# A decoder layer on one core: x fetched ahead of the modulation's weights, its transposes and the convolution's taps placed elsewhere

## The chip, the cores and the metric

The kernel runs as one program on one core of a Trainium2 chip. The measure is the device time of one execution in microseconds. Three runs of the kernel before gave 1677.51, 1674.44 and 1684.07 us, with a median of 1677.51 us. The execution that was profiled took 1679.29 us; its span, from the first to the last instruction in the trace, is 1677.5 us.

## The reference

One step of one decoder layer for 256 prompt rows and 64 sample rows (8 sequences of 8), 320 rows of 2048 numbers in all. Cut to what touches the change:

```python
ada = silu(c) @ w_ada + b_ada                 # c: 9 vectors of 2048; w_ada: 2048 x 12288
sh1, sc1, g1, sh2, sc2, g2 = split(ada, 6)
h = layer_norm(x) * (1 + sc1) + sh1           # x: 320 x 2048
proj = h @ w_in                               # w_in: 2048 x 7168
# S5 state-space branch and convolution branch (31 taps for each channel) on parts of proj,
# gates, an output product, a second norm, then a mixture of 32 experts, and a last norm
x = layer_norm(ALPHA * x + g1 * mix, ln1_g, ln1_b)
```

The modulation vectors `sc1` and `sh1` need 4096 of the 12288 columns of `w_ada` before `h` can be made; `layer_norm(x)` needs all of x.

## The kernel before, in words

Everything here is about the first 180 us. Work is written down as a program in Python; a scheduler then fixes the order of each engine's instructions from that order, from priorities and from its own estimate of times. On the chip each engine runs its list in that order and waits where an operand is not there.

**The four sets.** `ada_set` makes 512 columns of `sc1` and 512 of `sh1`. It reads 16 blocks of `w_ada`, 128 rows by 1024 columns, 0.524 MB each, issued on SP's queue as two DMAs of 256 KB (L279). Four matmuls at half width multiply a pair of blocks (helper line L188, tile `adp`), so a set is eight groups of two blocks; they are called group 1 to group 8 here, and the blocks of all sets are counted from 0, so that group 1 of the second set takes blocks 16 and 17. There are seven buffers for the blocks: four that rotate, named `raw`, two inside `rawu`, and `rawc`. The four `raw` buffers also hold the first slices of `w_in` (L601). A block is fetched when its buffer is free, and SP issues in the written order. At a set's end ScalarE copies `adp` out (`ae`, L304), four small products with `pair` fold it (tile `tpp`), and VectorE adds the bias into `ada` (L312).

**x.** `x_load` (L238 to L243) fetches x in three DMAs: two of 1.05 MB and one of 0.52 MB. They stand behind the first four blocks of `w_ada`. `ln0` first takes the statistics (L335) and normalises x in place (L338), then transposes it in 16 chunks of 128 columns (L346): three transposes on TensorE into a PSUM tile `s5p`, of which there are two, and one copy by ScalarE (L347) into `xnT`. The tiles of x lie in the same memory as the three big tables of the S5 setup, so that the first table (L418) waits for the last transposes.

**Beside them.** `s5_setup` makes the tables and small matrices of the S5 branch, mostly on VectorE. `taps` (L613 to L620) lays out the convolution's taps by 128 tiny matmuls from `cwn` into one `tpp` tile. `bias_rows` transposes the bias. `k_outer(k)` makes `h` of chunk k (L360 to L363, its high part on ScalarE at L368), fetches 768 columns of `w_in`, splits them in a high part (ScalarE, L542) and a low part (VectorE, L543), and multiplies them in 18 matmuls into six PSUM tiles (`acc`, `s5p`). It runs for chunks 4(q-1) to 4(q-1)+3 inside set q, and for 12 to 15 behind the last set. After that the products with `w_in` go on in blocks of 256 columns.

Of the kernel before, what the change touches and what calls it, by code (L numbers as in the profile page):

```python
# [24 lines left out]
T = SEQ + NB * TS  # L25
# [16 lines left out]
TOK = ((0, 128), (128, 128), (256, 64))  # L42
# [106 lines left out]
def bc(ap, shape):  # L149
    return ap.to_broadcast(shape)  # L150


def build(tc, A, O):
    nc = tc.nc
    V, S, GP, PE, SY = nc.vector, nc.scalar, nc.gpsimd, nc.tensor, nc.sync
# [19 lines left out]
    def acc():  # L175
        return pp.tile([128, 512], F32, name="acc", tag="acc", bufs=4)

    def s5p(name="s5p"):
        return pp.tile([128, 512], F32, name=name, tag="s5p", bufs=2)

    def tpp(name="tpp"):
        return pp.tile([128, 512], F32, name=name, tag="tpp", bufs=1)

    def stg(name="stg", shape=(128, T), dt=F32):
        return pa.tile(list(shape), dt, name=name, tag="stg", bufs=7)

    def mm(out, l, r, a, b, skip=True):
        return PE.matmul(out, lhsT=l, rhs=r, start=a, stop=b, skip_group_check=skip)  # L188
# [7 lines left out]
    ident = kc[:, C_ID:C_ID + 128]  # L196
# [41 lines left out]
    def x_load():  # L238
        for i, (t0, n) in enumerate(TOK):
            if i < 2:  # L240
                SY.dma_start(out=xt[i], in_=A["x_prompt"][0, t0:t0 + n])
            else:
                SY.dma_start(out=xt[i][:n], in_=A["x_sample"].rearrange("b s d -> (b s) d"))  # L243
# [4 lines left out]
    ps = tpp()  # L248
# [5 lines left out]
    def bias_rows():  # L254
        bn = stg("bn")
        S.dma_start(out=bn[:96, :128], in_=A["b_ada"][0].rearrange("(k p) -> k p", p=128))
        ps = tpp()
        PE.transpose(ps[:, :96], bn[:96, :128], ident[:96, :96])
        V.tensor_copy(bT, ps[:, :96])
        for part in (1, 4):  # L260
            V.tensor_scalar(bT[:, 16 * part:16 * part + 16], bT[:, 16 * part:16 * part + 16], 1.0, None, op0=OP.add)
# [30 lines left out]
    def ada_set(cols):  # L292


        ps = pp.tile([128, 512], F32, name="adp", tag="adp", bufs=1)
        for k in range(0, KT, 2):
            raws = [ada_load(cols, k + h) for h in range(2)]
            four([(ps[64 * a + 32 * h:64 * a + 32 * h + 32, :], scT[:, k + h, :], raws[h][:, 512 * a:512 * a + 512],
                   k == 0, k == KT - 2) for h, a in ((1, 1), (0, 0), (0, 1), (1, 0))])
            yield  # L300
            yield
        es = [stg("ae")[:, :256] for i in range(2)]
        for i, e in enumerate(es):
            S.copy(e, ps[:, 256 * i:256 * i + 256])  # L304
        yield
        tp = tpp()
        for i in range(4):
            mm(tp[:, 64 * i:64 * i + 64], es[i // 2][:, 128 * (i % 2):128 * (i % 2) + 128], pair, True, True)
        tv = tp[:, :256].rearrange("p (i a s) -> p a i s", i=4, a=2)
        for a, c in enumerate(cols):  # L310
            f = c // 128
            tt(ada[:, f:f + 4, :], tv[:, a, :, :NS], bc(bT[:, f:f + 4, None], [128, 4, NS]), op=OP.add)  # L312
        yield


    def rstd_(v, tmp, y):

        ts(v, v, EPS, None, op0=OP.add)
        root = S.activation(tmp, v, AF.Sqrt)
        V.reciprocal(y, tmp)  # L320
        tt(tmp, y, y, op=OP.mult)
        tt(tmp, tmp, v, op=OP.mult)
        ts(tmp, tmp, -0.5, 1.5, op0=OP.mult, op1=OP.add)
        tt(y, y, tmp, op=OP.mult)
        return root

    xnT = [pr2.tile([128, 8, T], F32, name=f"xnT{h}", tag=("Y0", "Y1")[h]) for h in range(2)]
    sdb = p0.tile([128, T], F32, name="sdb", tag="sdb")

    def ln0():  # L330
        st = stg("st")
        mv = stg("mv")
        for i, (t0, n) in enumerate(TOK):
            for c in range(4):
                V.bn_stats(st[:n, 24 * i + 6 * c:24 * i + 6 * c + 6], xt[i][:n, 512 * c:512 * c + 512])  # L335
            V.bn_aggr(mv[:n, 2 * i:2 * i + 2], st[:n, 24 * i:24 * i + 24].rearrange("p (c s) -> p c s", s=6))
            rstd_(mv[:n, 2 * i + 1:2 * i + 2], mv[:n, 16 + i:17 + i], mv[:n, 8 + i:9 + i])
            ts(xt[i][:n], xt[i][:n], mv[:n, 2 * i:2 * i + 1], mv[:n, 8 + i:9 + i], op0=OP.subtract, op1=OP.mult)  # L338

            stt(mv[:n, 24 + i:25 + i], mv[:n, 2 * i + 1:2 * i + 2], ALPHA, mv[:n, 8 + i:9 + i],  # L340
                op0=OP.mult, op1=OP.mult)
        yield
        for k in range(KT):
            ps = s5p()
            for i, (t0, n) in enumerate(TOK):
                PE.transpose(ps[:, t0:t0 + n], xt[i][:n, 128 * k:128 * k + 128], ident[:n, :n])  # L346
            S.copy(xnT[k // 8][:, k % 8, :], ps[:, :T])  # L347
            yield
        ps = tpp()
        for i, (t0, n) in enumerate(TOK):  # L350
            mm(ps[:, t0:t0 + n], bc(mv[:n, 24 + i:25 + i], [n, 128]), ident[:n, :n], True, True)
        V.tensor_copy(sdb, ps[:, :T])
        yield

    h_hi = pa.tile([128, KT, T], F32R, name="h_hi", tag="H0")
    h_lo = pa.tile([128, KT, T], F32R, name="h_lo", tag="H1")
# [241 lines left out]
    def k_outer(k):  # L598
        make_h(k)
        raw = raw_tile()  # L600
        SY.dma_start(out=raw[:, :768], in_=w_in[:, k, 0:768])  # L601
        hi, lo = split(raw[:, :768], 768)
        for m in range(6):
            mm3(first[m][:, :T], hi[:, 128 * m:128 * m + 128], lo[:, 128 * m:128 * m + 128],
                hh[0](k), hh[1](k), k == 0, k == KT - 1)
# [4 lines left out]
    def taps():  # L610
        ps = tpp()
        pick = ident[:CW, 0:32].rearrange("p (r s) -> p s r", s=4)
        for c in range(8):  # L613
            for j in range(4):
                x = 32 * c + 8 * j
                for s in range(4):
                    mm(ps[32 * s:32 * s + 32, x:x + 8], cwn[:CW, 128 * c + 32 * j:128 * c + 32 * j + 32], pick[:, s, :],
                       True, True)
        V.tensor_copy(cwS.rearrange("p c j r -> p (c j r)"), ps[:, :256])
        V.tensor_reduce(oneh, ident.rearrange("p (a c) -> p c a", a=4), axis=AX, op=OP.add)  # L620

    setup, norm = Side(s5_setup()), ln0()
    for q in range(4):
        for i, _ in enumerate(ada_set([D + 512 * q, 512 * q])):
            if q == 0:
                if i == 2:
                    x_load()
                    taps()
                if i == 3:
                    bias_rows()  # L630
                    next(norm)
                if 6 <= i < 15:
                    next(norm, None)
                    next(norm, None)
                setup.give(800)
            else:
                if i % 4 == 3 and i < 16:
                    k_outer(4 * q - 4 + i // 4)
                setup.give(1100)
# [906 lines left out]
    for c in range(4):  # L1546
        tv = [x.rearrange("p (f kk) -> p kk f", kk=4) for x in parts_of[c][:5]]
        for h in range(2):
            for kk in range(4):
                ps = acc()  # L1550
# [732 lines left out]
```

## Time and profile before

| what | value |
|---|---|
| median of three runs | 1677.51 us |
| profiled execution | 1679.29 us, span 1677.5 us |
| TensorE busy over the span | 1486.2 us, 89% |
| VectorE, ScalarE, GpSimd busy | 878.0, 550.3, 247.6 us |
| bytes over the span | 447.39 MB, mean 267 GB/s |
| mean busy share of the DMA engines, 40 to 60 us | 0.61 |
| the same, 120 to 140 us | 1.14 |

In the rows on engines the busy time of a stretch stands before the count of instructions in brackets. The DMA share is the mean over 16 engines and can pass 1 where transfers of several queues overlap. A row of a timeline gives the start, the time to the end of the last one, the engine, the line, the operation with out<-in, the number merged in the row, and in square brackets how long the engine had been idle and what ended that. TensorE records two matmuls for each 4-byte one that the program writes, so that a group of four is eight records.

### The profile page before, as it was taken

What the parts mean: (1) busy time and instruction counts of PE and PEld (TensorE: products, weight loads), DVE (VectorE), ACT (ScalarE), POOL (GpSimd) and SP (SyncE); (2) the same over time, 40 slices, a digit from 0 to 9 for tenths busy, and PEclk for the clock granted to TensorE, in tenths of its full rate; (3) what the DMA queues carried; (4) which work ended last, traced back from release to release, by engine and by line L of the source; (5) the groups of instructions that cost most, each with busy time, mean ns of one, the idle gap of its engine ahead of it and who ended that gap; (6) DMA issues with size and microseconds to landing.
All of it is one profiled execution on the core that took longest, in us unless ns stands there. A gap on an engine that the chain in (4) does not pass through costs nothing. (4 is left out here: it accounts for less than half of the span.)

```text
span 1677.5 us, 28072 instructions
## 1 busy us (share of the span) xinstructions
PE 1486.2 (89%) x10731; PEld 1039.7 (62%) x10731; DVE 878.0 (52%) x1724; ACT 550.3 (33%) x960; POOL 247.6 (15%) x419
## 2 busy tenths in 40 slices
PE   4977988998999899989799999989879997979894
PEld 1453877887777778878688988858522332323431
DVE  4564347675924853796354645463531533424365
ACT  1222433342324224523333433332231423232534
POOL 3021212134222210101100000000200000010013
PEclk9987989999999999999899999989999999989997
DMA  9799999789679976867576645555799899999992
GB/s 260 255 313 291 280 275 235 239 217 268 175 229 247 181 217 197 221 220 229 186 248 217 213 134 175 167 194 226 292 401 413 320 411 412 412 360 412 412 412 101
DMA packets 214899, 447.39 MB, mean 267 GB/s; under 512 B 23811, under 2 KB 134067, under 8 KB 206732
## 3 DMA queue, kind: packets, MB, share of 16 engines
q1 hardware_dynamic: 179572, 395.65, 67.8%
q0 software_dynamic: 29168, 43.15, 11.9%
q10 hardware_dynamic: 6016, 6.70, 1.3%
q8 instruction: 87, 1.43, 0.4%
q14 instruction: 56, 0.46, 0.1%
HBM read 425.53 MB, written 21.77 MB: 267 GB/s over the span
## 5 line engine op out<-in xcount | busy, mean ns | idle before, releaser
L543 DVE TENSOR_TENSOR wlo<-raw,whi 128x1024 fp32r<-128x1024 f32 (+1 forms) x196 | 237.6, 1213 | 304.0 <-ACT whi L542 298.8
L542 ACT CAST whi<-raw 128x1024 fp32r<-128x1024 f32 (+1 forms) x196 | 201.8, 1030 | 388.6 <-PE acc L188 231.9
L188 PE MATMUL acc<-h_hi,whi 128*128 128x320 f32 x864 | 275.9, 324 | 5.5 <-ACT whi L542 3.6
L188 PE MATMUL acc<-h_lo,whi 128*128 128x320 f32 x864 | 272.5, 318 | 0.0
L188 PE MATMUL acc<-h_hi,wlo 128*128 128x320 f32 x864 | 261.9, 322 | 5.3 <-DVE wlo L543 5.2
L188 PE MATMUL up<-ring,xg 128*32 128x512 f32 x1344 | 175.5, 610 | 11.1 <-DMA ring<-in_moe_w_gate 10.2
L188 PEld LDWEIGHTS acc<-h_hi,whi 128*128 128x128 f32 x864 | 167.3, 195 | 28.9 <-ACT whi L542 10.8
L188 PEld LDWEIGHTS acc<-h_hi,wlo 128*128 128x128 f32 x864 | 162.6, 194 | 22.1 <-DVE wlo L543 8.2
L188 PEld LDWEIGHTS acc<-h_lo,whi 128*128 128x128 f32 x864 | 167.7, 194 | 3.6 <-issue 1.4
L188 PE MATMUL adp<-raw,scT 128*32 128x512 f32 x636 | 120.7, 689 | 22.9 <-DMA raw<-in_w_ada 22.9
L188 PEld LDWEIGHTS up<-ring,xg 128*32 128x32 f32 x1344 | 42.6, 113 | 102.3 <-issue 90.3
L188 PE MATMUL pd<-ring,aT 128*32 128x512 f32 (+1 forms) x688 | 97.7, 675 | 5.9 <-DVE aT L1871 5.9
L188 PE MATMUL acc<-y_hi,whi 128*128 128x320 f32 x256 | 80.0, 315 | 6.6 <-DVE m L1010 6.6
L1927 ACT COPY z<-pd 32x512 f32<-32x512 f32 (+1 forms) x92 | 53.0, 576 | 87.3 <-PE pd L188 84.9
L1709 DVE TENSOR_TENSOR x1tok<-x1tok,acc 128x512 f32<-128x512 f32 x80 | 51.7, 683 | 56.6 <-PE acc L188 56.3
L188 PE MATMUL acc<-m_hi,whi 128*128 128x320 f32 x256 | 81.3, 319 | 0.0
L188 PE MATMUL acc<-m_lo,whi 128*128 128x320 f32 x256 | 80.2, 314 | 0.0
L188 PE MATMUL acc<-y_lo,whi 128*128 128x320 f32 x256 | 79.6, 313 | 0.0
L188 PE MATMUL acc<-m_hi,wlo 128*128 128x320 f32 x256 | 78.3, 317 | 0.0
L188 PE MATMUL acc<-y_hi,wlo 128*128 128x320 f32 x256 | 75.9, 316 | 0.0
L188 PE MATMUL acc<-vhl,whi 128*128 128x320 f32 x256 | 58.5, 324 | 2.1 <-DVE vhl L915 2.1
L1610 DVE COPY xg<-XS 128x512 f32 x34 | 14.5, 426 | 84.8 <-PE up L188 81.6
(689 smaller groups left out, 2581.2 us busy)
## 6 DMA issues: line engine op xcount, KB each, us to landing
ring<-in_moe_w_up SPq DMA_DIRECT2D x120, 512.0 KB, 11.5
ring<-in_moe_w_gate SPq DMA_DIRECT2D x120, 512.0 KB, 11.5
ring<-in_moe_w_down SPq DMA_DIRECT2D x60, 1024.0 KB, 11.6
raw<-in_w_ada SPq DMA_DIRECT2D x119, 512.0 KB, 5.3
raw<-in_w_in SPq DMA_DIRECT2D x100, 512.0 KB, 5.8
raw<-in_w_ada SPq DMA_DIRECT2D x80, 256.0 KB, 5.1
raw<-in_w_out SPq DMA_DIRECT2D x32, 512.0 KB, 4.5
rawu<-in_w_ada SPq DMA_DIRECT2D x32, 256.0 KB, 5.1
```

The lines of the kernel that those rows point to most:

```text
L188: return PE.matmul(out, lhsT=l, rhs=r, start=a, stop=b, skip_group_check=skip)
L542: S.copy(hi[:, :n], raw_ap)
L543: tt(lo[:, :n], raw_ap, hi[:, :n].bitcast(F32), op=OP.subtract)
L1610: state[g % 2] = (V.tensor_copy if g % 2 == 0 else S.copy)(xg[:, :, 32 * g:32 * g + 32], XS[:, :, bass.ds(off, 32)])
L1709: tt(x, x, o, op=OP.add)
L1927: S.copy(zs[q * ng + nb][0][s0:s0 + m_], pd[m_ * q:m_ * q + m_])
```

## The change

The call of `x_load` moves ahead of the four sets, so SP issues x before any block of `w_ada`. The order of the other DMAs on SP's queue stays. In `ln0` the three products that spread the rows' scale (`sdb`) move ahead of the transposes and lose their own step. In the first set the statistics are taken at step 2 rather than 3, one chunk is asked for at each of the steps 4 to 15 (two at each of 6 to 14 before), and the last four chunks are written in the second set's steps 0 to 4. `taps` is written behind the last group of the first set (step 16).

```diff
         yield
+        ps = tpp()
+        for i, (t0, n) in enumerate(TOK):
+            mm(ps[:, t0:t0 + n], bc(mv[:n, 24 + i:25 + i], [n, 128]), ident[:n, :n], True, True)
+        V.tensor_copy(sdb, ps[:, :T])
         for k in range(KT):
             ...
             S.copy(xnT[k // 8][:, k % 8, :], ps[:, :T])
             yield
-        ps = tpp()
-        for i, (t0, n) in enumerate(TOK):
-            mm(ps[:, t0:t0 + n], bc(mv[:n, 24 + i:25 + i], [n, 128]), ident[:n, :n], True, True)
-        V.tensor_copy(sdb, ps[:, :T])
-        yield
...
+    x_load()
     setup, norm = Side(s5_setup()), ln0()
     for q in range(4):
         for i, _ in enumerate(ada_set([D + 512 * q, 512 * q])):
             if q == 0:
                 if i == 2:
-                    x_load()
-                    taps()
+                    next(norm)
                 if i == 3:
                     bias_rows()
-                    next(norm)
-                if 6 <= i < 15:
+                if 4 <= i < 16:
                     next(norm, None)
-                    next(norm, None)
+                if i == 16:
+                    taps()
                 setup.give(800)
             else:
+                if q == 1 and i < 5:
+                    next(norm, None)
```

On VectorE all twelve statistics of x now stand ahead of the S5 setup's first operations; before, those stood ahead. The copy `sp<-tpp` of the setup, which needs a transpose that TensorE makes behind group 1, now stands between the first and the second of the three normalisations.

TensorE inside the first set, before: two transposes of a chunk, a group, and the first transposes of the chunks behind it (`xt_95` to `xt_97` are the three tiles of x).

```order
L346 MATMUL s5p<-kc,xt_96 128x128
L346 MATMUL s5p<-kc,xt_97 128x64
L188 MATMUL adp<-rawu,scT 32x512
L188 MATMUL adp<-raw,scT 32x512 x2
L188 MATMUL adp<-rawu,scT 32x512
L346 MATMUL s5p<-kc,xt_95 128x128
L346 MATMUL s5p<-kc,xt_96 128x128
L346 MATMUL s5p<-kc,xt_97 128x64
L346 MATMUL s5p<-kc,xt_95 128x128
L346 MATMUL s5p<-kc,xt_96 128x128
L346 MATMUL s5p<-kc,xt_97 128x64
```

The same place with the change:

```order
L188 MATMUL tpp<-kc,cwn 32x8 x13
L350 MATMUL s5p<-kc,xt_95 128x128
L188 MATMUL adp<-rawu,scT 32x512
L188 MATMUL adp<-raw,scT 32x512 x2
L188 MATMUL adp<-rawu,scT 32x512
L350 MATMUL s5p<-kc,xt_96 128x128
L350 MATMUL s5p<-kc,xt_97 128x64
L188 MATMUL tpp<-kc,cwn 32x8 x11
L350 MATMUL s5p<-kc,xt_95 128x128
L350 MATMUL s5p<-kc,xt_96 128x128
L350 MATMUL s5p<-kc,xt_97 128x64
L188 MATMUL tpp<-kc,cwn 32x8 x15
```

The tiny matmuls of the taps (`cwn`), which stood between groups 1, 2 and 3 before, now stand between the chunks from group 3 on, up to group 7. All sixteen chunks stand ahead of group 8 of the first set; before, fifteen did, and the last one behind it.

TensorE from the end of the first set into the second, before: the folding products with `pair`, groups 1 to 4 of the second set, then the first matmuls of chunk 0 (`h_hi,whi`).

```order
L188 MATMUL tpp<-pair,ae 128x64 x4
L188 MATMUL adp<-rawu,scT 32x512
L188 MATMUL adp<-raw,scT 32x512 x2
L188 MATMUL adp<-rawu,scT 32x512 x2
L188 MATMUL adp<-raw,scT 32x512 x2
L188 MATMUL adp<-rawu,scT 32x512
L188 MATMUL adp<-rawc,scT 32x512
L188 MATMUL adp<-raw,scT 32x512 x2
L188 MATMUL adp<-rawc,scT 32x512
L188 MATMUL adp<-raw,scT 32x512 x4
L188 MATMUL acc<-h_hi,whi 128x320 x4
L188 MATMUL s5p<-h_hi,whi 128x320 x2
```

With the change, from group 8 of the first set on:

```order
L188 MATMUL adp<-raw,scT 32x512 x4
L188 MATMUL tpp<-pair,ae 128x64 x4
L188 MATMUL adp<-rawu,scT 32x512
L188 MATMUL adp<-raw,scT 32x512 x2
L188 MATMUL adp<-rawu,scT 32x512 x2
L188 MATMUL adp<-raw,scT 32x512 x2
L188 MATMUL adp<-rawu,scT 32x512
L188 MATMUL acc<-h_hi,whi 128x320 x4
L188 MATMUL s5p<-h_hi,whi 128x320 x2
L188 MATMUL adp<-rawc,scT 32x512
L188 MATMUL adp<-raw,scT 32x512 x2
L188 MATMUL adp<-rawc,scT 32x512
```

The first six matmuls of chunk 0 now stand ahead of group 3, and twelve more of them ahead of group 4.

TensorE at the end of the fourth set, before: group 7, the folding products of the third set, group 8, and chunk 8 of `k_outer`.

```order
L188 MATMUL adp<-rawc,scT 32x512
L188 MATMUL adp<-raw,scT 32x512 x2
L188 MATMUL adp<-rawc,scT 32x512
L188 MATMUL tpp<-pair,ae 128x64 x4
L188 MATMUL adp<-raw,scT 32x512 x4
L188 MATMUL acc<-h_hi,whi 128x320 x4
L188 MATMUL s5p<-h_hi,whi 128x320 x2
L188 MATMUL tpp<-pair,ae 128x64 x4
L188 MATMUL acc<-h_lo,whi 128x320
```

With the change, from group 6 of the fourth set on:

```order
L188 MATMUL adp<-rawu,scT 32x512
L188 MATMUL adp<-raw,scT 32x512 x2
L188 MATMUL adp<-rawu,scT 32x512
L188 MATMUL tpp<-pair,ae 128x64 x4
L188 MATMUL acc<-h_hi,whi 128x320 x4
L188 MATMUL s5p<-h_hi,whi 128x320 x2
L188 MATMUL adp<-rawc,scT 32x512
L188 MATMUL adp<-raw,scT 32x512 x2
L188 MATMUL adp<-rawc,scT 32x512
L188 MATMUL acc<-h_lo,whi 128x320
L188 MATMUL acc<-h_hi,wlo 128x320
L188 MATMUL acc<-h_lo,whi 128x320
```

The folding products of the third set and the first matmuls of chunk 8 now stand ahead of group 7; group 8 stands behind all of chunks 8 and 9.

## Rows read from the trace of the kernel before

**Rows 1.** Windows of 20 us: busy (count) by engine, clock, DMA share, GB/s.

```profile
0.00:20.00 20.00, 5.96 (x86) 2.00 (x89) 4.25 (x24) 3.18 (x4) 13.49 (x23) 1.00 0.91 236
...
40.00:60.00 20.00, 20.00 (x74) 7.18 (x73) 0.75 (x2) 6.30 (x16) 0.00 (x0) 1.00 0.61 206
60.00:80.00 20.00, 16.55 (x85) 9.79 (x85) 19.96 (x28) 3.71 (x8) 0.00 (x0) 0.83 0.87 292
...
120.00:140.00 20.00, 12.72 (x75) 4.90 (x74) 3.21 (x4) 3.38 (x6) 4.05 (x7) 0.75 1.14 337
```

**Rows 2.** Waits of SP's queue, 0 to 200 us: total us, times, longest.

```profile
SPq L279 <- PE adp L188: 41.3, 21, 4.9
```

**Rows 3.** Timeline of TensorE and VectorE, 17 to 38 us, arrivals and statistics.

```profile
17.73 1.06 PE L188 MATMUL adp<-rawu,scT 128*32 128x512 f32 x1 [5.21 <-DMA rawu<-in_w_ada]
...
20.41 1.88 DVE L335 BATCH_NORM_STATS2 st<-xt 128x6 f32<-128x512 f32 x3 [5.69 <-DMA xt<-in_x_prompt]
...
25.33 0.69 DVE L335 BATCH_NORM_STATS2 st<-xt 128x6 f32<-128x512 f32 x1 [1.93 <-DMA xt<-in_x_prompt]
...
29.87 1.27 DVE L335 BATCH_NORM_STATS2 st<-xt 64x6 f32<-64x512 f32 x2
...
30.68 1.06 PE L188 MATMUL adp<-rawc,scT 128*32 128x512 f32 x1 [1.75 <-DMA rawc<-in_w_ada]
...
36.47 1.33 DVE L338 TENSOR_SCALAR xt<-xt,mv 64x2048 f32<-64x2048 f32 x1
```

**Rows 4.** Timeline of TensorE, 11 to 62 us.

```profile
11.04 0.42 PE L397 MATMUL tpp<-kc,misc 96*128 96x96 f32 x1
...
19.59 2.42 PE L188 MATMUL tpp<-kc,cwn 31*32 31x8 f32 x166
...
38.32 0.80 PE L188 MATMUL tpp<-kc,mv 128*128 128x128 f32 x2
...
41.74 3.73 PE L346 MATMUL s5p<-kc,xt 128*128 128x128 f32 x12
...
45.39 1.06 PE L188 MATMUL adp<-rawu,scT 128*32 128x512 f32 x1
...
57.35 1.93 PE L188 MATMUL adp<-raw,scT 128*32 128x512 f32 x8
...
60.13 1.97 PE L188 MATMUL tpp<-pair,ae 128*128 128x64 f32 x8
```

**Rows 5.** Timelines of VectorE, ScalarE and SP's queue, 59 to 73 us.

```profile
59.73 2.29 DVE L418 TENSOR_TENSOR ta__401<-w,kc 128x2048 f32<-128x2048 f32 x1 [19.25 <-PE s5p L346]
...
68.38 0.95 DVE L543 TENSOR_TENSOR wlo<-raw,whi 128x768 fp32r<-128x768 f32 x1
...
69.35 0.33 SPq L601 DMA_DIRECT2D raw<-in_w_in  x1
69.78 0.85 SPq L279 DMA_DIRECT2D raw<-in_w_ada  x2
...
70.63 1.54 ACT L368 CAST h_hi<-h 128x320 fp32r<-128x320 f32 x4 [7.00 <-DVE h L363]
...
72.09 1.11 SPq L279 DMA_DIRECT2D raw<-in_w_ada  x2
```

**Rows 6.** Timeline of TensorE, 65 to 123 us: the same forms at different speeds.

```profile
65.55 0.62 PE L188 MATMUL adp<-rawc,scT 128*32 128x512 f32 x1
...
86.82 1.07 PE L188 MATMUL adp<-raw,scT 128*32 128x512 f32 x8 [1.28 <-DMA raw<-in_w_ada]
...
113.25 1.12 PE L486 MATMUL tpp<-kc,padB 128*128 128x128 f32 x4
...
122.54 0.66 PE L486 MATMUL tpp<-kc,padB 128*128 128x128 f32 x4
```

**Rows 7.** Timeline of TensorE, 156 to 158 us, end of the fourth set.

```profile
156.76 1.07 PE L188 MATMUL adp<-raw,scT 128*32 128x512 f32 x8 [1.31 <-DMA raw<-in_w_ada]
157.76 0.85 PE L188 MATMUL acc<-h_hi,whi 128*128 128x320 f32 x4
```

## The prediction

> **What bounds the kernel now.** I read the windows of 20 us first, then the waits of SP's queue, then the timelines of the first 160 us engine by engine, because the change touches nothing behind them. The reader is to see two limits that take turns. From 60 us on the DMA engines are busy 0.87 of the time, and later all of it (a share of 1.14 from 120 to 140): the weights of the four sets, 64 blocks or 33.6 MB, come as fast as they can. Between 40 and 60 us it is the other way round: TensorE has no idle time at all, 20.00 of 20 us, and the DMA engines stand at 0.61, so 7.8 us of DMA time lie unused there [rows 1]. The link between the two is the seven buffers: SP waits 41.3 us in 21 pieces for TensorE to let go of a block [rows 2]. So a group that TensorE takes late is a fetch that starts late, and where the DMA engines are full a late fetch is never made good. What the change is worth is read from two things: when the first set's folding products run (60.13 us, [rows 4]), and whether the fetches behind them find a gap.
>
> TensorE is slow in all of this stretch. [...] The clock column of the windows says 1.00 there [rows 1]; the durations are what I go by.
>
> **Term A, the end of the first set.** The bytes are the same, only their order differs, so I take arrival from how many bytes SP's queue had landed at four moments before: 2.10 MB (group 2) at 17.73, 3.15 MB (first tile of x) at 20.41, 4.19 MB (second tile) at 25.33, 5.77 MB (group 3) at 30.68 [rows 3]. With x first, its second tile has the place of group 2, 17.7 us; all of x (2.62 MB) is there by 19.1, group 1 (3.67 MB) at 22.9, group 2 (4.72 MB) at 27.1, group 3 at 30.7 as before.
>
> VectorE: one statistic takes 0.63 us (three in 1.88). Four on the second tile end at 20.2, four on the third at 22.7. From there to the last normalisation before, 31.14 to 37.80, were 6.7 us with the S5 setup's small operations between; three normalisations alone are 4.0 us [rows 3]. So x is ready between 26.7 and 29.4 us, against 37.8 before. The setup's copy that now stands between the normalisations waits for group 1 and a transpose, 22.9 + 1.9 + 0.4 = 25.2 us, which lies inside that.
>
> TensorE has the chunks behind group 2, which ends at 27.1 + 1.9 = 29.0 us. So the chunks start at 29.0, where most of them started at 41.74 before, and this looks like a gain of several us. It isn't one, because what stood in TensorE's idle time before now stands behind that point too. The work from there to the end of group 8: 16 chunks at 0.91 us (four from 41.74 to 45.39) are 14.6; six groups at 1.9 are 11.4; the taps, 256 records at the pace of 166 in 2.42, are 3.7; the scale's three products 1.2; the bias's transpose, by the like one at 11.04, 0.4 [rows 4]. The sum is 31.3 us, and TensorE has no wait in it that I can find: group 3 is there at 30.7, and a pair of blocks needs 3.6 us at the 292 GB/s of rows 1, less than the 5 us that TensorE spends on a group with its chunks. Group 8 so ends at 60.3. Behind it ScalarE's copy and the start of the folding products take 0.85 us (59.28 to 60.13 before, filled then by the last chunk, which now stands ahead). They start at 61.2 against 60.13: **+1.0 us**. Of the 3.7 us for the taps nothing is hidden any more; without them the term would be -2.7. Its bounds: x ready at the early end, with group 2 no later, gives 26.7 + 31.3 + 0.85 - 60.1 = -1.3; group 2 as late as group 3 was, since GpSimd's loads now fall together with x, gives 30.7 + 1.9 + 31.3 + 0.85 - 60.1 = +4.6.
>
> That the transposes spread over two sets is only true of the text: in TensorE's order all sixteen chunks stand ahead of group 8 of the first set. Were four of them behind it, A would be 3.7 us less.
>
> **Term B, the second set.** Groups 3 and 4 now stand behind matmuls of chunk 0. These need h, and h comes off VectorE late: before, the first table of the setup started at 59.73 and ScalarE's high part of h came at 70.63, 10.9 us later, while group 3 had run at 65.55 [rows 5, 6]. With the change the table starts when the last chunk is copied, about 58.4, but the addition of the bias waits for the folding products, which end near 63.1; that is 1.0 us earlier than 64.1 before, when two tables (2.2 us each) stood ahead. The low part of the weights, 0.9 us, moves behind h. So h is there at about 70.6 - 1.0 - 0.9 = 68.7. Six matmuls take 1.2 us at the pace of four in 0.85 [rows 7], group 3 another 1.9, and ends near 72.0 instead of 66.6. Block 24 waits for its buffer: it was issued at 69.78, behind the slice of `w_in` at 69.35, and is now issued at 72.0. Twelve more matmuls (2.4 us) and group 4 (1.9) follow, to 76.5; block 26, issued at 72.09 before, waits for that: 4.4 us later [rows 5]. Behind it on SP's queue is every later block. Not all of it is lost: between 60 and 80 us the DMA engines already had 0.13 x 20 = 2.6 us idle [rows 1], and this is the same idle time made longer. I take 4.4 - 2.6 = **+1.8 us**, between 0 (the queue still holds enough) and +4.4. The third set has a like place, chunk 4 ahead of its groups 3 and 4; there h is nearer, since the tables are done: **+0.5**, between 0 and +4.4.
>
> **Term C, the end of the fourth set.** Chunk 8 started at 157.76 behind group 8, which had waited 1.31 us for its blocks [rows 7]. Now chunks 8 and 9 stand ahead of group 8, and that wait is filled with their work: **-1.3 us**, between 0 and -3.8 (all of chunk 8 done while the blocks come: 18 matmuls at 0.85 / 4).
>
> **The sum** is 1.0 + 1.8 + 0.5 - 1.3 = +2.0 us. Behind 160 us the same work follows on TensorE, so I carry it to the end. The profiled execution, 1679.29 us (span 1677.5 and 1.8 around it), becomes 1681.3; it stood 1.8 above the median of 1677.51, so the forecast is **1679.5 us**.
>
> **The rivals.** (1) TensorE reaches its upper level inside the first set. Against it: the 20 us from 40 to 60 were without a gap before, with the same groups and chunks, and every group still took 1.9 us [rows 1, 4]. For it: the taps now stand in between. Behind group 4, four groups would save 0.86 each, and ten chunks 41% of 0.91 (transposes of one form take 1.12 and 0.66, [rows 6]): 3.4 + 3.7 = 7.1, so +2.0 - 7.1 = -5.1, 1672.4 us. More than the 7.8 us of idle DMA time can't come of it, which gives 1671.7; with A and C at their far ends 1666.9. [...]
>
> (2) Slower: the fetches run dry. Chunk 0 ahead of groups 3 and 4 holds two buffers, block 26 comes 4.4 us late, the DMA engines find nothing to do and the loss stays, and again in the third set, while C brings nothing since the last blocks come later by as much: 1.0 + 4.4 + 4.4 = +9.8, 1687.3 us. It decides when block 26 is issued later than about 78 us, or when the idle DMA time between 60 and 100 us grows by more than 5 us. For it: the DMA engines are full from 80 us on. Against it: the 2.6 us already idle, and groups that were waiting for data rather than for TensorE (1.28 us at 86.82, [rows 6]).
>
> **How the numbers follow.** A measurement of this kernel can tell about 0.5%, 8.4 us, from no change: below 1669.1 is faster, above 1685.9 slower. My forecast has 0.58; all four terms at their ends at once would give 1672.4 and 1690.9, and its own range is 1674 to 1686, so it is nearly all "same" (0.54), with 0.03 slower and 0.01 faster. Rival 1 has 0.22, of which 0.14 is faster, since its far end and a start before group 4 pass the line. Rival 2 has 0.20, of which 0.17 is slower. That makes 0.15 faster, 0.65 same, 0.20 slower. The range from 1669 to 1688 leaves out the tails of both rivals.
>
> **What would show it.** A: group 2 near 27 us, the chunks from about 29, the folding products of the first set within 1 us of 61; the taps between 35 and 56 us, not in idle time. If the groups in there take 1.1 us, rival 1 is right. B: ScalarE's `h_hi` near 69, group 3 of the second set behind it near 70 to 72, and the fetch behind the second slice of `w_in` issued 2 to 3 us later than at 69.78; a DMA share well under 0.87 between 60 and 80 would speak for rival 2. C: chunk 8 ahead of group 7 of the fourth set, no wait before group 8. I am wrong outright if x comes so much earlier that the chunks start by 24 us, or if the end of the first set moves by more than 5 us either way.

## The result: slower by 1%

The changed kernel takes 1695.14 us in the median of 13 runs (1683.04 to 1701.51), the kernel before 1681.01 in 13 runs beside it (1669.79 to 1688.36). The ratio is 1.010, with a 95% interval from 1.0073 to 1.0127: +14 us, outside the forecast's range. The profiled execution of the changed kernel is one of its quick ones (1685.44 us, span 1683.6), so its span understates the loss; its first 200 us don't. A marker near 190 us, the first `us` copy behind the projection, comes 13.0 us late. The first row is of the kernel before, the second of the changed kernel (timeline of ScalarE):

```profile
180.35 0.42 ACT L646 COPY uf<-acc 128x320 f32<-128x320 f32 x1
```

```profile
193.34 0.42 ACT L647 COPY uf<-acc 128x320 f32<-128x320 f32 x1
```

**The first set.** ScalarE and VectorE of the changed kernel, 3 to 34 us:

```profile
3.48 0.29 ACT L247 ACTIVATE cN<-cN 16x128 f32<-16x128 f32 x1
...
12.50 2.47 DVE L335 BATCH_NORM_STATS2 st<-xt 128x6 f32<-128x512 f32 x4 [2.01 <-DMA xt<-in_x_prompt]
...
22.37 0.35 ACTq L256 DMA_DIRECT2D bn<-in_b_ada  x1
22.75 1.28 ACT L319 ACT_TABLE_LOAD   x1 [18.98 <-DMA rawu<-in_w_ada]
24.05 0.20 ACT L319 ACTIVATE mv<-mv 128x1 f32<-128x1 f32 x1
24.36 2.44 DVE L335 BATCH_NORM_STATS2 st<-xt 64x6 f32<-64x512 f32 x4
...
31.86 1.33 DVE L338 TENSOR_SCALAR xt<-xt,mv 64x2048 f32<-64x2048 f32 x1
```

ScalarE does nothing between 3.8 and 22.4 us. It is held at the issue of the 48 KB bias load. ScalarE's instructions in the order of the program, with the semaphore that each one waits for (the wait of L246 for `DMAHW1_49` ends, in the changed kernel's trace, with the landing of `cN`, after 0.80 us), cut to the lines around the issue, of the kernel before and then of the changed kernel:

```
1 L195 DMA kc<-in_kc 128x192
2 L256 DMA bn<-in_b_ada 96x128
3 L246 ACT_TABLE_LOAD
4 L246 ACTIVATE cN<-cN 128x128 [waits DMAHW1_49]
```

```
3 L246 ACTIVATE cN<-cN 128x128 [waits DMAHW1_49]
4 L247 ACTIVATE cN<-cN 16x128 [waits DMAHW2_49]
5 L256 DMA bn<-in_b_ada 96x128 [waits DMAHW1_49]
6 L319 ACT_TABLE_LOAD
```

The issue now stands behind the activations and waits for the semaphore that L246 waits for; by the trace the 18.98 us ahead of L319 ended with the landing of a block of weights (`rawu`). The square root for x's first tile can run only behind it, and the third tile's statistics stand behind that root's use in VectorE's order. So x, whose second tile is there at 12.50, is ready at 31.86 + 1.33 = 33.2 us.

TensorE of the changed kernel, 33 to 66 us, beside [rows 4]:

```profile
33.24 0.47 PE L350 MATMUL s5p<-kc,xt 64*128 64x64 f32 x2 [0.82 <-DMA rawu<-in_w_ada]
...
35.04 1.06 PE L188 MATMUL adp<-rawc,scT 128*32 128x512 f32 x1
...
40.50 0.69 PE L188 MATMUL tpp<-kc,cwn 31*32 31x8 f32 x34
...
42.76 1.94 PE L188 MATMUL adp<-raw,scT 128*32 128x512 f32 x8
...
63.07 1.93 PE L188 MATMUL adp<-raw,scT 128*32 128x512 f32 x8
...
65.58 1.97 PE L188 MATMUL tpp<-pair,ae 128*128 128x64 f32 x8 [0.57 <-ACT ae L304]
```

From 33.24 us TensorE has nearly no gap, every group takes 1.9 us (one takes 1.03 at 95.87 in the same trace), and the folding products come at 65.58, 5.4 us after those of [rows 4]. These two paces of one form, 1.9 us and 1.0 to 1.1, are what is called the lower and the upper level from here on.

**The sets behind.** ScalarE, TensorE and SP's queue, 73 to 81 us, beside [rows 5, 6]:

```profile
73.22 1.54 ACT L367 CAST h_hi<-h 128x320 fp32r<-128x320 f32 x4 [2.27 <-DVE h L362]
73.73 0.85 PE L188 MATMUL acc<-h_hi,whi 128*128 128x320 f32 x4 [2.61 <-ACT h_hi L367]
...
76.74 0.81 SPq L279 DMA_DIRECT2D raw<-in_w_ada  x2
...
79.34 1.06 PE L188 MATMUL adp<-raw,scT 128*32 128x512 f32 x8
...
80.50 1.11 SPq L279 DMA_DIRECT2D raw<-in_w_ada  x2
```

Chunk 0 stands ahead of groups 3 and 4 and waits for h. Block 24 goes out at 76.74 (69.78 before), block 26 at 80.50 (72.09). The waits of SP's queue for TensorE grow from 41.3 [rows 2] to 60.0 us:

```profile
SPq L279 <- PE adp L188: 60.0, 21, 5.9
```

The windows of the changed kernel (columns as in [rows 1]), and behind them the one of the kernel before that [rows 1] leave out:

```profile
40.00:60.00 20.00, 20.00 (x314) 9.79 (x316) 1.49 (x7) 4.39 (x11) 0.00 (x0) 1.00 0.49 161
60.00:80.00 20.00, 16.82 (x80) 7.27 (x72) 16.91 (x26) 4.72 (x10) 0.00 (x0) 0.91 0.80 254
80.00:100.00 20.00, 15.80 (x95) 11.33 (x92) 14.45 (x17) 7.32 (x7) 0.43 (x1) 0.83 0.79 260
```

```profile
80.00:100.00 20.00, 15.26 (x95) 8.97 (x95) 17.61 (x34) 8.61 (x9) 1.80 (x1) 0.90 0.92 320
```

The idle DMA time from 40 to 100 us grows from (0.39 + 0.13 + 0.08) x 20 = 12.0 us to (0.51 + 0.20 + 0.21) x 20 = 18.4. At the end of the fourth set (TensorE, beside [rows 7]):

```profile
165.45 0.85 PE L188 MATMUL acc<-h_hi,whi 128*128 128x320 f32 x4 [1.95 <-ACT h_hi L367]
...
172.11 1.06 PE L188 MATMUL adp<-raw,scT 128*32 128x512 f32 x8
```

Group 8 no longer waits, but it comes 15.3 us after that of [rows 7]. The two are not at the same place of the order: in the changed kernel chunks 8 and 9 stand ahead of it. Group 6 stands ahead of chunk 8 in both kernels, and it comes 12.7 us later (first row before, second changed):

```profile
148.65 1.06 PE L188 MATMUL adp<-rawu,scT 128*32 128x512 f32 x1 [0.38 <-DMA rawu<-in_w_ada]
```

```profile
161.39 0.62 PE L188 MATMUL adp<-rawu,scT 128*32 128x512 f32 x1
```

### The profile page after: what moved, and what is told of

Same layout as the page of the kernel before. It is cut to its first block, busy times and chain, and to the rows that moved or that the text cites. A ratio compares the mean times of both kernels' runs of the same rounds, so it can differ in the third digit from the quotient of the medians.

```text
span 1683.6 us, 28071 instructions
## 1 busy us (share of the span) xinstructions
PE 1491.1 (89%) x10731; PEld 1039.0 (62%) x10731; DVE 879.2 (52%) x1724; ACT 552.0 (33%) x960; POOL 247.3 (15%) x419
## 5 line engine op out<-in xcount | busy, mean ns | idle before, releaser
L188 PE MATMUL adp<-raw,scT 128*32 128x512 f32 x636 | 124.4, 699 | 12.9 <-DMA raw<-in_w_ada 12.9
L188 PE MATMUL adp<-rawu,scT 128*32 128x512 f32 x88 | 32.8, 832 | 33.6 <-DMA rawu<-in_w_ada 33.6
```

## The experiments

One table first, since the text under it speaks of its columns. The first three are times in the profiled execution: the first set's folding products, group 8 of the fourth set, the first `us` copy. The ratio is to the kernel before on the same chip, with its 95% interval. Each edit is small in the program, but the scheduler's order for TensorE changes beyond the place that it names. So the group 8 column is not like for like: ahead of that group stand chunks 0 to 7 in the kernel before, taps_back, x_first_alone, dense_products, dense_timed and before_dense, chunk 8 and a part of 9 too in bias_first and taps_late_alone, all of 8 and 9 in the changed kernel and bias_and_taps, and 8 to 10 in the other four.

| kernel | folding | group 8 | us copy | ratio |
|---|---|---|---|---|
| before, twice | 60.1, 59.4 | 156.8, 159.4 | 180.4, 184.0 | 1 |
| changed, twice | 65.6, 65.3 | 172.1, 173.2 | 193.3, 197.0 | 1.010 (1.0073 to 1.0127) |
| bias_first | 48.6 | 155.1 | 175.5 | 1.002 (0.9982 to 1.0059) |
| taps_back | 54.2 | 152.2 | 177.4 | 1.0045 (1.0015 to 1.0076) |
| chunk0_late | 65.7 | 166.8 | 186.0 | 1.0078 (1.0044 to 1.0112) |
| x_first_alone | 53.0 | 154.7 | 184.6 | 1.0015 (0.9976 to 1.0054) |
| bias_and_taps | 53.8 | 154.8 | 177.4 | 1.0041 (1.0005 to 1.0077) |
| bias_and_chunk0 | 49.4 | 152.1 | 170.9 | 0.9951 (0.9919 to 0.9982) |
| taps_late_alone | 65.3 | 159.5 | 179.9 | 1.0011 (0.9985 to 1.0037) |
| bias_pool | 52.0 | 152.2 | 171.6 | 0.9948 (0.9913 to 0.9983) |
| bias_and_chunks | 48.7 | 152.3 | 174.9 | 1.002 (0.9986 to 1.0054) |
| dense_products, dense_timed | 57.0, 57.5 | 154.2, 157.4 | 179.4, 183.1 | 1.002 (0.9991 to 1.0049) |
| before_dense | 52.1 | 153.4 | 181.1 | 1.0015 (0.9988 to 1.0042) |

**bias_first** (the edit shortened)

```
-        bn = stg("bn"); S.dma_start(out=bn, in_=b_ada)    # in bias_rows(), step 3
+    bn = stg("bn"); S.dma_start(out=bn, in_=b_ada)        # ahead of the activations
```

> The changed kernel with one edit: the 48 KB bias load is issued at the program's start, ahead of ScalarE's activations, instead of behind them. Theory H (the held engine): in the changed kernel ScalarE stood from 3.8 to 22.4 us at the issue of this load, so the square roots, x's third statistics and the transposes came late, and TensorE, solid from 33.2 us, reached the first set's last products at 65.6 instead of 60.1. By H the square roots go by 14 us, the transposes start before group 2, and the last products come at about 61.8 (group 2's landing 27.1 plus some 35 us of TensorE work that is left behind it); the first us copy, 193.3 in the changed kernel, comes at about 189.5, and the median is 3 to 5 us under the changed kernel's, ratio to the kernel before about 1.006. Rival R (x first in itself: the weights land behind 2.5 MB, and the fetches run short until the end of the fourth set): the last products come no earlier than 64.5, the first us copy not before 192, ratio 1.010.

H's place was right and its size far too small: the folding products came 17.0 us earlier, not 3.8. ScalarE, VectorE and TensorE of this kernel:

```profile
1.18 0.46 ACTq L237 DMA_DIRECT2D bn<-in_b_ada  x1
...
11.48 0.20 ACT L319 ACTIVATE mv<-mv 128x1 f32<-128x1 f32 x1 [6.46 <-DVE mv L318]
...
27.68 1.33 DVE L338 TENSOR_SCALAR xt<-xt,mv 64x2048 f32<-64x2048 f32 x1
...
30.10 0.62 PE L188 MATMUL adp<-rawc,scT 128*32 128x512 f32 x1
...
47.00 1.07 PE L188 MATMUL adp<-raw,scT 128*32 128x512 f32 x8
48.63 1.10 PE L188 MATMUL tpp<-pair,ae 128*128 128x64 f32 x8 [0.57 <-ACT ae L304]
```

The last normalisation ends at 29.0 instead of 33.2 us: 4.2 us is what the hold itself cost x. The rest goes with the pace: from group 3 on TensorE is at its upper level (a group takes 1.1 us, 1.9 in the changed kernel), and from group 3 to the folding products it needs 18.5 us where the changed kernel needed 30.5 (35.04 to 65.58). That this level could be had in the first set theory H had not said. No run takes the hold away and leaves the level low, so what the 4.2 us alone cost in time is not shown.

**taps_back**

```
                 if i == 2:
+                    taps()
                     next(norm)
-                if i == 16:
-                    taps()
```

> The changed kernel with one edit: the taps are called at step 2 of the first set again, as in the kernel before. In the changed kernel the taps' nine pieces take 4.7 us between 40.5 and 57.6, inside the stretch in which TensorE is solid. Theory T (the taps' place): the last products of the first set come 4.7 us earlier, at about 60.9, since TensorE was idle before 33 us; the first us copy at about 189, the ratio to the kernel before about 1.006. Theory H (the held engine) allows the same 4.7 at most, since the bias load stays behind the activations and the transposes still start at 29.5. Rival R (x first in itself): the last products may come earlier, but the first us copy stays at 192 or later, since the weights' landing times set it; ratio 1.010.

11.4 us earlier, more than the 4.7 that T and H allowed: here too TensorE reaches the upper level (a group takes 1.9 us at 41.21 and 1.1 at 45.45), with the bias load as late as in the changed kernel (22.01 us). Rival R is wrong in both runs. A group of this kernel in the first set:

```profile
45.45 0.62 PE L188 MATMUL adp<-rawu,scT 128*32 128x512 f32 x1
```

**chunk0_late**

```
+                if q == 1 and i == 7:
+                    k_outer(0)
-                if i % 4 == 3 and i < 16:
+                if i % 4 == 3 and i < 16 and (q, i) != (1, 3):
```

> The changed kernel with one edit: chunk 0 of the projection is called at step 7 of the second set instead of step 3, which puts groups 3 and 4 of that set ahead of chunk 0 on TensorE again, as in the kernel before; the first set is untouched. Theory B (chunk 0 ahead of the groups): in the changed kernel groups 3 and 4 of the second set came 9.3 us later than before though the first set ended only 5.4 later, and blocks 24 and 26 were issued 7.0 and 8.4 later; with the groups back ahead the first set's last products stay at 65.6, groups 3 and 4 come at 71 and 75.5 (5.4 later than before), block 26 is issued at about 77.5, and the first us copy comes at about 189; ratio 1.007. Rival (a delay of the first set is passed on whatever the order, and the rest comes from the fetches that were put off by it): group 6 of the second set still stands for a fetch, the first us copy stays between 192 and 194, ratio 1.010.

Theory B holds as far as block 26: group 4 of the second set comes at 74.25 and block 26 at 77.70 (TensorE and SP's queue), as forecast. The marker moves from 193.3 and 197.0 to 186.0, but the last fetches don't: the last two blocks of the fourth set (third, fourth and fifth row: this kernel, the changed kernel, the kernel before) go out when they did in the changed kernel. The order of the third and fourth sets came out differently, too, so what chunk 0's place alone costs behind block 26 stays open. In the time it is 0.2%, within the two intervals.

```profile
74.25 1.07 PE L188 MATMUL adp<-raw,scT 128*32 128x512 f32 x8 [1.57 <-DMA raw<-in_w_ada]
...
77.70 0.81 SPq L279 DMA_DIRECT2D raw<-in_w_ada  x2
...
160.15 3.75 SPq L279 DMA_DIRECT2D raw<-in_w_ada  x4
```

```profile
160.35 3.03 SPq L279 DMA_DIRECT2D raw<-in_w_ada  x4
```

```profile
147.31 4.16 SPq L279 DMA_DIRECT2D raw<-in_w_ada  x4
```

**x_first_alone** (the kernel before)

```
+    x_load()
     setup, norm = Side(s5_setup()), ln0()
...
-                    x_load()
                     taps()
```

> The kernel before with one edit: x is fetched ahead of the modulation's weights; the taps, the folding products and the steps at which the transposes are called stay. By this the bias load goes out ahead of the activations, and the taps stand in TensorE's order before group 3. Theories H, T and B together (the harm lies in the held ScalarE, in the taps' late place and in chunk 0's place, not in x's early fetch): TensorE has some 27 us of work from group 3 (about 30.5) to the last products of the first set, which come at about 57.5 instead of 60.1; the first us copy comes at 178 to 181 and the ratio is 0.997 to 1.001. Rival R (x first in itself): the last products come at 61 or later, the first us copy at 188 or later, ratio 1.007 or more.

The folding products come at 53.0 and the time is unchanged: R is wrong for the first set. So fetching x first costs nothing measurable in itself; here, where the bias load goes out early and the taps stand early, it brings nothing either. But the marker came at 184.6, later than H had it; the 7 us won by 53 us were gone by 185.

**bias_and_taps** (both edits above)

> The changed kernel with two edits that each brought the first set's last products forward when made alone (65.6 us in the changed kernel; 48.6 with the bias load issued first, 54.2 with the taps back at step 2): both together. Theory L (a level of the clock and then the weights' landing: either edit lets TensorE reach its upper level inside the first set, and behind 50 us the weights' landing decides, so the gains don't add): last products at 46 to 50, first us copy at 173 to 178 (175.5 and 177.4 for the single edits), ratio to the kernel before 1.000 to 1.004. Rival S (the two costs are separate and add): last products at about 37 to 40, first us copy at about 160, ratio 0.993.

Theory L: the gains don't add (53.8, 177.4, 1.0041). The folding products were later than L's 46 to 50, since the level rose only at about 46 us here (a group takes 1.9 us at 44.23 and 1.1 at 48.40).

**bias_and_chunk0** (bias_first with chunk0_late)

> The changed kernel with the bias load issued first (first us copy 175.5 instead of 193.3) and chunk 0 called at step 7 of the second set, behind groups 3 and 4 (by itself 186.0 instead of 193.3). Theory B (the order of the second set has a cost of its own, blocks fetched late): the 7.3 us come on top, first us copy at about 168, ratio 0.998. Rival L (behind 50 us the weights' landing decides): first us copy 174 to 177, ratio 1.002 as with the bias load alone.

Nearer to B: 170.9, and with a ratio of 0.9951 it beats both kernels. So the order behind the first set costs on its own. That it is the second set's is not shown: chunks 8 to 10 stand ahead of group 8 of the fourth set here, which is not so in bias_first.

**taps_late_alone** (the kernel before, `taps()` at step 16)

> The kernel before with one edit: the taps are called at step 16 of the first set, which puts their products between the transposes; x and the bias load stay as they were. Theory T: their 3.7 to 4.7 us, hidden in TensorE's idle time before, stand in its solid stretch: the first set's last products come at 64 to 65 instead of 60.1, the first us copy at 184 to 186, ratio 1.002 to 1.003. Rival L (the level of the clock decides, and the order of the products sets it): the last products come at 57 or earlier, if TensorE reaches its upper level, and the groups in the first set take 1.1 us instead of 1.9.

Neither. The folding products came at 65.3 as T had it, but not by T's mechanism: in the middle of the set TensorE was at its upper level (second row; a group takes 1.1 us), with taps between the transposes, and behind a stall of 4.0 us (third row) it was at the lower one again (1.9 us at 60.05). So taps in that place didn't keep the level down. And the late folding products cost nothing: the marker came at 179.9, earlier than T's 184 to 186, with a ratio of 1.0011. Groups 1 to 3 of the second set stand ahead of the folding products here and come at 60.0 to 63.5 us, no later than in the kernel before (62.0 to 65.5).

```profile
38.80 1.06 PE L188 MATMUL adp<-rawu,scT 128*32 128x512 f32 x1
...
43.28 0.62 PE L188 MATMUL adp<-rawu,scT 128*32 128x512 f32 x1
...
56.86 0.99 PE L346 MATMUL s5p<-kc,xt 128*128 128x128 f32 x3 [3.98 <-ACT xnT L347]
```

**before_again and after_again** (unchanged)

> The kernel before, unchanged, a second time. If what the first 200 us show belongs to the kernel and not to one execution, the first set's last products come within 1 us of 60.1, the first us copy within 2 us of 180.4, the groups before them take 1.9 us again, and the rest of the execution holds the difference of the two spans. If the clock's level in the first set is a matter of the single execution, the last products differ by more than 5 us.

> The changed kernel, unchanged, a second time. If the first set belongs to the kernel, its last products come within 1 us of 65.6 again with groups of 1.9 us, and the first us copy within 4 us of 193.3 (the kernel before varied by 3.6 between two executions). If the low level in the first set was a matter of that one execution, the last products come at 55 or earlier.

The first set repeats within 0.8 us, at the lower level in all four executions (1.9 us a group). The marker repeats within 3.7, where I had expected 2 for the kernel before; of the mean of two it is 182.2 before and 195.2 after, 13.0 apart.

**bias_pool**

```
-        S.dma_start(out=bn[:96, :128], ...)
+        GP.dma_start(out=bn[:96, :128], ...)
```

> The changed kernel with one edit: the bias load goes out on GpSimd's queue instead of ScalarE's, at the same place of the program, so that it is no earlier there than GpSimd's other loads and ScalarE holds no issue. TensorE's order follows: the taps now stand between groups 7 and 8 of the first set, and chunk 0 behind groups 3 and 4 of the second. Theory H (what cost the time is that ScalarE was held at the issue): the first square root runs at about 11 us instead of 24, the last products of the first set come at 47 to 50, the first us copy at 169 to 174, ratio to the kernel before 0.995 to 0.998. Rival (the bias had to be there early, and that is what the earlier load brought): the last products stay at 60 or later, ratio 1.006 or more.

H: a bias that is no earlier in the program, but issued from GpSimd, so that ScalarE holds no issue, gives 52.0 (forecast 47 to 50), 171.6 and 0.9948, which beats both kernels as well. TensorE's order differs too: chunk 0 stands behind the groups here, and the taps stand between groups 5 and 8 of the first set. ScalarE's first root:

```profile
10.71 0.20 ACT L319 ACTIVATE mv<-mv 128x1 f32<-128x1 f32 x1 [5.81 <-DVE mv L318]
```

**bias_and_chunks** (bias_first, the first chunk of each later set at step 7)

> The changed kernel with the bias load issued first, and with the first chunk of the projection called at step 7 instead of step 3 in the second, third and fourth set (with the second set's alone: first us copy 170.9, ratio 0.995). Theory B (a chunk that needs late work, put ahead of the groups, delays fetches in each set): another 2 to 4 us, first us copy 167 to 169, ratio 0.993. Rival L (the blocks' landing decides from here): first us copy 170 to 174, ratio 0.995.

No gain over chunk 0's move alone: 174.9 and 1.002, if anything worse. Theory B doesn't carry to the third and fourth set, and the 0.5% of bias_and_chunk0 hangs on the order of the later sets, too.

**dense_products and dense_timed**

```
+                if i == 5:
+                    ps = s5p()
+                    for _ in range(3):
+                        mm(ps, ident, scT.rearrange("p k b -> p (k b)"), True, True)
```

> The changed kernel with work added: three products of 128x128 by 128x512 that nobody reads, at step 5 of the first set, ahead of group 3, where TensorE is at its lower level; the bias load stays as it is. Theory L (the level decides where the first set ends): TensorE reaches its upper level by about 45 us, the groups behind take 1.0 to 1.1 us instead of 1.9, and the last products come at 54 to 60, earlier than the 65.6 of the changed kernel though there is more to do. Rival W (the amount of work and its start decide): the products add their 4 to 5 us, and the last products come at 69 to 71.

> The changed kernel with three products that nobody reads ahead of group 3 of the first set, timed (one look gave 57.0 us for the first set's last products and 179.4 for the first us copy). Theory L (most of what the change lost was the lower level of TensorE's clock in the first set): the ratio to the kernel before is 1.000 to 1.005, like those of the two kernels that reached the upper level by another edit (1.002 and 1.0045). Rival (what happens in the first 200 us is taken back or added to behind them): 1.008 to 1.011, as the changed kernel.

The test of the level by itself: nothing is taken away, 4.9 us of products that nobody reads are put in (first row), and the set ends 8.6 us earlier; a group takes 1.9 us ahead of them (27.48) and 1.1 behind them. TensorE:

```profile
33.94 4.92 PE L188 MATMUL s5p<-scT,kc 128*128 128x512 f32 x6
38.79 0.62 PE L188 MATMUL adp<-rawc,scT 128*32 128x512 f32 x1
...
54.83 1.07 PE L188 MATMUL adp<-raw,scT 128*32 128x512 f32 x8
...
56.97 1.10 PE L188 MATMUL tpp<-pair,ae 128*128 128x64 f32 x8
```

The time falls with it, from 1.010 to 1.002, though ScalarE is held as before (the bias load goes out at 22.19 us). So W is wrong, and raising the level goes with taking back most of the change's loss. The level is not what sets the two kernels apart, since the kernel before runs its first set at the lower level as well (1.9 us a group). And in this run the order of the second and the fourth set fell back to that of the kernel before, with chunk 0 behind groups 3 and 4 and group 8 ahead of chunk 8, so a part of the 0.8% may be that.

**before_dense** (the same products in the kernel before, at step 7)

> The kernel before with the same three products added at step 7 of the first set, which puts them behind group 5, in the stretch from 40 to 60 us where TensorE is solid at its lower level; x, the taps and the bias load stay. Theory L (the level, and not x's early fetch, is what can be gained in the first set): the upper level comes by 48 us, the last products at 55 to 58 instead of 59.4 to 60.1 though 4.9 us of work are added, the first us copy at 176 to 180 (180.4 and 184.0 in the kernel before), ratio 0.996 to 1.000. Rival W (the products cost what they take): last products at 64 to 65, first us copy at 185 or later, ratio 1.003.

The level rises (a group takes 1.9 us at 38.06 and 1.1 at 44.55) and the folding products come at 52.1, 7 us or more earlier. By group 8 of the fourth set 3 to 6 us of it are left, at the marker nothing (181.1), and the time doesn't move. The level in the first set is worth nothing to the kernel before; x first with the bias load and chunk 0 put right (bias_and_chunk0, bias_pool) is worth 0.5%.

```profile
39.93 4.27 PE L188 MATMUL s5p<-scT,kc 128*128 128x512 f32 x6
...
52.12 1.10 PE L188 MATMUL tpp<-pair,ae 128*128 128x64 f32 x8
```

## Why the prediction was wrong

**Term A was mis-sized because of one step: "x is ready between 26.7 and 29.4 us".** It was ready at 33.2. I had followed x's bytes and VectorE's work, and not what ScalarE does for x; an issue that had moved behind the activations and got a wait of its own held it until 22.4 us. Without the hold the step is right: 29.0 us in bias_first. Everything behind it was counted well: from 33.24 to 65.58 are 32.3 us, against 31.3 + 0.85 in the prediction. So A was +5.4 instead of +1.0, past its bound of +4.6, and the end of the first set moved by more than the 5 us that the prediction names as its sign of being wrong.

**Terms B and C together were +7.5 us at the marker instead of +1.0.** Block 26 was forecast 15.3 us behind the folding products (76.5 less 61.2) and came 14.9 behind them (80.50 less 65.58), so B's mechanism was right as far as that. But I let 2.6 us of idle DMA time swallow a part, gave the third set 0.5, and had C give some back. From the folding products to group 6 of the fourth set, which stands behind chunks 0 to 7 and ahead of chunk 8 in both kernels, the lag grew from 5.4 to 12.7 us, 7.3 where B and the third set had 2.3; from there to the marker it grew by 0.2, where C had -1.3 within 0 and -3.8. The second executions of the two kernels share it out otherwise (lags of 6.0, 8.4 and 13.0 us, so 2.4 and 4.6), with a sum of 7.0. In both, C brings nothing: chunks 8 and 9 do fill the wait of group 8, as forecast, and the marker gains nothing by it. Rival 2 had said this, that the loss stays, that it comes again in the third set and that C brings nothing: its two times 4.4 make 8.8, and block 26 passed its mark of 78 us. Its other sign, 5 us more of idle time between 60 and 100 us, was just missed (4.2 to 8.2). How much of the 7.5 us is chunk 0's place is open, since in chunk0_late the last blocks go out no earlier. With A's 5.4 that is, but for rounding, the 13.0 us of the marker, and the medians say 14.

**Rival 1 did not come true, and its level was the hinge all the same.** The level did not rise, as I had it at 0.78 (a group took 1.93 us at 63.07). The rival's 0.86 us a group is about what the runs show (1.94 at 42.76 in the changed kernel, 1.06 at 34.38 in bias_first). But I took it for a side case with a price: every edit that let TensorE reach the upper level in the first set brought the folding products to 57.5 us or earlier, but for taps_late_alone, which was at the lower level again by 60.05. Why the loss shows and the gain hardly does is only in part in the table: folding products anywhere between 48.6 and 60.1 give a group 8 of the fourth set between 152 and 159; at 65.6, with chunk 0 ahead of the groups, it is 172. I put the first down to the DMA engines, which are full from 120 to 140 us (a share of 1.14 in [rows 1], 1.20 in the changed kernel); no run tests that by itself. And it is not the folding products that must be early: at 65.3 in taps_late_alone, behind the second set's first groups, they cost nothing.

**Open.** What raises the level is not shown: the kernel before has groups at 36.45 and 39.87 with products between them and stays low (1.9 us at 45.39), taps_late_alone has a like stretch, with groups at 35.13 and 38.80, and rises (1.1 us at 43.28). The changed kernel, with groups, transposes and taps and hardly a gap, stayed low for 32 us (33.24 to 65.58), and bias_first reached the upper level with the same transposes; no run tests transposes or taps by themselves. And kernels with a marker 5 to 7 us ahead of the kernel before (bias_first, bias_and_taps) are not faster in time; the interval of bias_and_taps even lies above 1, as does that of taps_back. What takes it back behind 190 us I did not find, single executions of one kernel being 1% and more apart.

## What to carry to other kernels

In these traces the issue of a load stands in the order of an engine's own work (here ScalarE's: issue at 22.37 us, the root behind it at 24.05, and at 11.48 in bias_first): when loads change places, look for an issue that has got a wait, and for what stands behind it on that engine, even if the load itself is small. Before a stretch at a slow pace is priced (1.9 us a group here), ask whether a small edit can give the quick one (1.1); in bias_first that was worth about three times the 4.2 us of the hold at the end of the first set, though the time shows much less of it. Where a later stage is full of fetches, price an early and a late finish in front of it apart: here early ones left a ratio between 0.995 and 1.0045, and a late one that held back the next fetches cost 0.8 to 1%. And measure a lag at a place that stands at the same point of the order in both kernels, or what was moved ahead of it is counted as delay.

## What I had not expected of the hardware

Adding 4.9 us of products made a stage 8.6 us shorter (dense_products). The clock column of the windows reads 1.00 from 40 to 60 us in both kernels, while groups take 1.9 us there, and 1.00 in taps_back too, where they take 1.9 us at 41.21 and 1.1 from 45.45 on; only the durations show the level in the first set. That it is a level of the clock, as my expectations call it, no run shows. And the issue of a 48 KB load, behind a wait, left ScalarE idle for 18.6 us.
